# Half of the K tiles of a ConvGLU's gate and value products formed by seven products, with seven operands made once from h

## The chip, the cores and the metric

One core of one Trainium2 chip runs the whole program once per execution. The metric is the device time of that execution in microseconds (us), lower is better. Everything is fp32 at the interface; the matrix products run on TensorE in a reduced fp32 form (fp32r), so each operand is first split into a high part and a low part.

## The reference, cut to what matters

One layer of a hybrid encoder on a sequence of 512 positions with 2048 features. The change touches its last third, the feed-forward network with a convolved gate:

```python
h   = rms_norm(x, norm2_g)                      # (512, 2048)
gv  = h @ ffn_w_up                              # (2048, 2*5504): gate columns, then value columns
g   = dwconv3(gv[..., :5504], dw_w, dw_b)       # width 3 along the positions
val = gv[..., 5504:]
x   = x + (gelu(g) * val) @ ffn_w_down          # (5504, 2048)
return rms_norm(x, final_g)
```

Ahead of it stand a projection, a spatial gating unit, a long convolution by FFT as matrix products, and the output projection `w_out` (`out_group`), whose last two quarters produce x.

## The kernel before, in words

**Products.** `mm3` (L222 to L226) forms one exact product as three matmuls: high by high (L224), high by low (L225, the other way round where the weights stream), low by high (L226). Weights arrive by DMA on SyncE's queue (SP) as raw fp32 tiles of 128x1024 (512 KB, or 384 KB for the last group); ScalarE (ACT) casts each to its high part `hi` (L143), VectorE (DVE) subtracts to get its low part `lo` (L144). `hi` and `lo` have three buffers each, and `next_unit` splits the unit that comes two later when a unit starts (`split_to(i + 3)`), so the split of a unit cannot begin before the unit three places ahead of it has left TensorE (PE), and has to be done two units later.

**Units.** The feed-forward part works in 11 groups of 4 tiles of 128 features (the last has 3). A list, `ffn_order` (L96 to L107), written out by loops, sets the order of the units; PE, ACT, DVE and SP all follow it.

- **R** ("regular"): two K tiles of h times 4 feature tiles of the gate or of the value: 24 matmuls of 512 columns. Eight R units make the gate of one group, eight the value. They accumulate in four PSUM banks `pa`.
- **S**: the product with `ffn_w_down` for the previous group, by a scheme of seven products in place of eight (Strassen's, in Winograd's form): 14 units of 12 matmuls of 512 columns, in two halves of seven. `prepare_to` forms the sums of weight quarters in place on DVE (L180), four buffers `sraw` hold the quarters. The operands `aH`/`aL` are made from the group's activations (`operands`, L1131 to L1169, in three pieces). After each unit `down_out` (L1193) copies two banks to a tile `cs` (ACT, L1199, three buffers) and POOL (GpSimd) issues one DMA, for the fourth unit of a half three, which adds `cs` to the DRAM tile `xd` (L1202, 512 KB each).
- **L**: the last group's product with `ffn_w_down`, direct, at the end.

In a group the R and S units alternate, so that PE gets 5.4 us of R behind nearly every S. Between two gate halves stand `gate_out` (L1121: four DVE multiplications of PSUM by the row `r2`, 1/rms of each position) and the pieces of the convolution (`conv_piece`: ACT L1112, two DVE operations L1113 and L1114, ACT Gelu L1115, and a multiplication by `r2` on POOL, L1116); behind a value half `value_out` (L1128: four DVE multiplications of the gate by PSUM) and the three pieces of `operands`.

**End.** Behind the last R the last S units run, then the L units; `load_fin` (L1280) fetches `xd` back, `last_out` (L1294 to L1297) adds it to the L result, squares and scales it, `leave` writes out.

Of the kernel before, what the change touches and what calls it, by code (L numbers as in the profile page):

```python
# [35 lines left out]
QUARTER = {0: ("11", 0, 0), 1: ("12", 0, 1), 2: ("22", 1, 1), 5: ("21", 1, 0)}  # L36
# [3 lines left out]
    ("11", "22", "11"), ("21", None, None), ("21", "21", "22"),  # L40
)

# [9 lines left out]
def encoder_kernel(ctx: ExitStack, tc: tile.TileContext, a: dict, out: bass.AP):  # L52
# [41 lines left out]

    ffn_order = []
    for gi in range(len(groups)):  # L96
        S = [("S", gi - 1, i // 7, i % 7) for i in range(14)] if gi else []
        G, V = ([("R", kind, gi, k0) for k0 in range(0, KD, 2)] for kind in ("gate", "value"))
        ffn_order += G[:3]
        for i in range(5):  # L100
            ffn_order += S[i : i + 1] + G[3 + i : 4 + i]
        ffn_order += S[5:7]
        late = 2 if gi == last else 0
        for i in range(5 - late):
            ffn_order += V[i : i + 1] + S[7 + i : 8 + i]
        ffn_order += V[5 - late :] + S[12 - late :]
# [40 lines left out]

    def load(i):
        e = plan[i]
        if e[0] == "S":  # L150
            _, gi, dp, u = e
            if u in QUARTER:
                name, ks, dh = QUARTER[u]
                raw = special["raw"]()
                j0, q = groups[gi][0], dp + 2 * dh
                rows = w_dn[j0 * P : (j0 + 4) * P, q * 512 : (q + 1) * 512]
                SP.dma_start(raw, rows.rearrange("(k s p) c -> p s k c", s=2, p=P)[:, ks])
                sraws[gi, dp, name] = raw
# [23 lines left out]

    def split_to(n):
        while st_["split"] < min(n, len(plan)):
# [6 lines left out]
            else:  # L191
                nk, n_ = (2, 512) if plan[i][0] == "S" else (plan[i][2], plan[i][4])
# [644 lines left out]
    xas = [kp.tile([P, 4, L], F32, tag="xa", name="xa", bufs=4) for _ in range(4)]  # L837

    def xa(k):
        return xas[k // 4][:, k % 4, :]  # L840
# [181 lines left out]
    def norm2(q):  # L1022
        H, Lo = h2[q]
        if q == 0:
            ss2s.append(const.tile([P, L], F32, tag="acc", name="ss2", bufs=1))
        ss2 = ss2s[0]
        for f in range(4):
            k = 4 * q + f
            split_scaled(H[:, f, :], Lo[:, f, :], xa(k), col("norm2", k))
            sq = (bo if q < 3 else A3).tile([P, L], F32, tag="ev", name="sq2", bufs=4 if q < 3 else 2)  # L1030
            square_into(ss2, xa(k), sq, k == 0)
# [16 lines left out]
    h2.append(h2_tiles(A2, 0))  # L1048
# [5 lines left out]
    for q in range(1, 4):  # L1054
        go_to(8 * q + 2)
        load_res()
        norm2(q - 1)
        if q < 3:
            h2.append(h2_tiles(A2, q))
# [3 lines left out]
    h2.append(h2_tiles(A3, 3))  # L1063

# [7 lines left out]
    special["raw"] = lambda: ff.tile([P, 2, 512], F32, tag="sraw", name="sraw", bufs=4)  # L1072
# [16 lines left out]
    def turn_x(k):  # L1089
# [6 lines left out]
        if k % 4 == 3:  # L1096
            for t in range(NT):
                SP.dma_start(
                    xd[q, t].rearrange("p (k c) -> p k c", k=4), xas[q][:, :, t * P : (t + 1) * P]
                )  # L1100

    ps_of = {}
    gg = {}
# [4 lines left out]
    def conv_piece(gi, f):  # L1108

        w0, w1, w2_, b = (col(*n(groups[gi][0] + f)) for n in fw)  # L1110
        e, d = gg[gi][:, f, :], tmp[f % 2]
        ACT.activation(d, e, AF.Identity, bias=b, scale=w1)  # L1112
# [319 lines left out]
```

## Time and profile before

| what | value |
|---|---|
| time, median of 3 runs | 2100.76 us (2098.84 to 2101.2) |
| the profiled execution's own time | 2101.48 us |
| its span, first to last instruction | 2099.7 us |
| PE busy | 2065.5 us, 98% of the span |
| DVE busy | 1218.8 us, 58% |
| ACT busy | 898.3 us, 43% |
| POOL busy | 406.7 us, 19% |
| mean granted TensorE clock | 0.995 of full speed |

The span is cut off at the first and last instruction; 1.8 us of the execution's own time lie around it. Busy shares are means over stages with different limits, and matmuls overlap each other in the records, so the time that PE needs for one is read from start to start, not from the recorded length. In every row, "idle" and an arrow name what the engine waited for before the instruction. In the numbers of lines, L1128 is line 1128 of the kernel before.

### The profile page before, as it was taken

What the parts mean: (1) busy time and instruction counts of PE and PEld (TensorE: products, weight loads), DVE (VectorE), ACT (ScalarE), POOL (GpSimd) and SP (SyncE); (2) the same over time, 40 slices, a digit from 0 to 9 for tenths busy, and PEclk for the clock granted to TensorE, in tenths of its full rate; (3) what the DMA queues carried; (4) which work ended last, traced back from release to release, by engine and by line L of the source; (5) the groups of instructions that cost most, each with busy time, mean ns of one, the idle gap of its engine ahead of it and who ended that gap; (6) DMA issues with size and microseconds to landing.
All of it is one profiled execution on the core that took longest, in us unless ns stands there. A gap on an engine that the chain in (4) does not pass through costs nothing.

```text
span 2099.7 us, 23963 instructions
## 1 busy us (share of the span) xinstructions
PE 2065.5 (98%) x9374; PEld 1711.0 (81%) x9374; DVE 1218.8 (58%) x1366; ACT 898.3 (43%) x1230; POOL 406.7 (19%) x304
## 2 busy tenths in 40 slices
PE   8999999999999999999999999999999999999996
PEld 6888887888888888888888888888888888888884
DVE  6873565556897944654555554465555555564555
ACT  6433542223544443543444443443444445344543
POOL 0330211100003510311313122131311213131220
PEclk9999999999999999999999999999999999999998
DMA  8434233243223463887868788786887868788886
GB/s 291 136 120 140 81 91 91 81 140 118 93 91 129 153 180 90 185 190 163 194 143 193 176 181 182 156 195 159 193 189 162 187 153 191 164 188 180 182 195 184
DMA packets 172413, 331.13 MB, mean 158 GB/s; under 512 B 10539, under 2 KB 26091, under 8 KB 170380
## 3 DMA queue, kind: packets, MB, share of 16 engines
q1 hardware_dynamic: 118000, 225.13, 32.9%
q0 software_dynamic: 48960, 94.38, 28.8%
q10 hardware_dynamic: 5340, 10.10, 1.4%
q8 instruction: 73, 1.20, 0.2%
q14 instruction: 40, 0.33, 0.0%
HBM read 222.61 MB, written 106.95 MB: 157 GB/s over the span
## 4 chain that ended last, share of the span: by engine, by line
PE 89%; DVE 6%; DMA 2%; ACT 1%; issue 1%; POOL 0%; SPq 0%; ACTq 0%; POOLq 0%; DVEq 0%
PE pa L224 19%; PE pa L226 19%; PE pa L225 19%; PE po L225 2%; PE po L224 2%; PE po L226 2%; PE se L226 2%; PE se L224 2%; PE se L225 2%; PE sa L226 2%; PE sa L224 2%; PE sa L225 2%; PE sc L226 2%; PE sc L225 2%; PE sc L224 2%; PE pv L224 1%
## 5 line engine op out<-in xcount | busy, mean ns | idle before, releaser
L144 DVE TENSOR_TENSOR lo<-raw,hi 128x1024 fp32r<-128x1024 f32 (+2 forms) x289 | 362.9, 1258 | 403.7 <-ACT hi L143 402.5
L224 PE MATMUL pa<-h2H,hi 128*128 128x512 f32 x1376 | 536.7, 390 | 0.0
L226 PE MATMUL pa<-h2H,lo 128*128 128x512 f32 x1376 | 535.6, 389 | 0.0
L225 PE MATMUL pa<-h2L,hi 128*128 128x512 f32 x1376 | 535.4, 389 | 0.0
L143 ACT CAST hi<-raw 128x1024 fp32r<-128x1024 f32 (+2 forms) x289 | 299.2, 1036 | 386.6 <-PE pa L225 233.4
L1202 POOL DMA_DIRECT2D xd<-cs x180 | 224.6, 1414 | 959.5 <-ACT cs L1199 797.4
L144 DVE TENSOR_TENSOR lo<-sraw,hi 128x1024 fp32r<-128x1024 f32 x140 | 199.0, 1421 | 332.3 <-ACT hi L143 332.2
L143 ACT CAST hi<-sraw 128x1024 fp32r<-128x1024 f32 x140 | 147.2, 1051 | 369.1 <-PE pa L225 367.7
L226 PEld LDWEIGHTS pa<-h2H,lo 128*128 128x128 f32 x1376 | 258.3, 188 | 53.8
L225 PEld LDWEIGHTS pa<-h2L,hi 128*128 128x128 f32 x1376 | 258.3, 188 | 53.3
L224 PEld LDWEIGHTS pa<-h2H,hi 128*128 128x128 f32 x1376 | 258.3, 188 | 53.2
L224 PE MATMUL pa<-hH,hi 128*128 128x512 f32 x512 | 203.3, 397 | 3.5 <-ACT hi L143 1.9
L225 PE MATMUL pa<-hL,hi 128*128 128x512 f32 x512 | 201.4, 393 | 0.0
L226 PE MATMUL pa<-hH,lo 128*128 128x512 f32 x512 | 200.5, 393 | 0.9 <-DVE lo L144 0.9
L224 PEld LDWEIGHTS pa<-hH,hi 128*128 128x128 f32 x512 | 97.1, 190 | 29.6 <-DVE ev L615 4.6
L226 PEld LDWEIGHTS pa<-hH,lo 128*128 128x128 f32 x512 | 97.2, 190 | 22.5 <-DVE lo L144 1.7
L225 PEld LDWEIGHTS pa<-hL,hi 128*128 128x128 f32 x512 | 97.3, 190 | 19.1
L180 DVE TENSOR_TENSOR sraw<-sraw 128x1024 f32<-128x1024 f32 x80 | 99.1, 1239 | 13.0 <-DMA sraw<-in_ffn_w_down 11.0
L1116 POOL TENSOR_TENSOR gg<-gg,r 128x512 f32<-128x512 f32 x43 | 71.6, 1832 | 65.5 <-ACT gg L1115 65.5
L1199 ACT COPY cs<-se 128x512 f32<-128x512 f32 x80 | 47.1, 589 | 51.5 <-PE se L226 51.5
L224 PE MATMUL sa<-hi,aH 128*128 128x512 f32 x160 | 62.2, 389 | 0.0
L225 PE MATMUL sa<-lo,aH 128*128 128x512 f32 x160 | 62.2, 389 | 0.0
(274 smaller groups left out, 3084.2 us busy)
## 6 DMA issues: line engine op xcount, KB each, us to landing
xd<-cs POOLq DMA_DIRECT2D x180, 512.0 KB, 7.8
raw<-in_ffn_w_up SPq DMA_DIRECT2D x160, 512.0 KB, 5.9
sraw<-in_ffn_w_down SPq DMA_DIRECT2D x80, 512.0 KB, 4.6
raw<-in_w_in SPq DMA_DIRECT2D x79, 512.0 KB, 3.7
raw<-in_w_out SPq DMA_DIRECT2D x32, 512.0 KB, 3.7
raw<-in_ffn_w_up SPq DMA_DIRECT2D x16, 384.0 KB, 5.6
xn<-in_xN ACTq DMA_DIRECT2D x8, 512.0 KB, 5.0
khat_d<-kh SPq DMA_DIRECT2D x4, 1024.0 KB, 4.4
```

Of the source, the lines that this page charges most:

```text
L143: ACT.copy(hi, src)
L144: eng.tensor_tensor(lo, src, f32(hi), ALU.subtract)
L180: DVE.tensor_tensor(raws[i], sraws[gi, dp, of], sraws[gi, dp, less], ALU.subtract)
L224: PE.matmul(o, ah, bh, start=start, stop=False, skip_group_check=read)
L225: PE.matmul(o, ah, bl, start=False, stop=False, skip_group_check=read)
L226: PE.matmul(o, al, bh, start=False, stop=stop, skip_group_check=read)
L1116: POOL.tensor_tensor(e, e, r2[0], ALU.mult)
L1199: ACT.copy(st[:, tp, :], chains[dp, CHAIN[u]][tp])
L1202: POOL.dma_start(dst, st, accum_op=ALU.add)
```

## The change

Of the 16 K tiles of h, the first 8 (`KS = 8`) are taken out of the R units. For them gate and value are formed by the same seven-product scheme as the down product, in new units **U**, seven for the gate and seven for the value of each group. A U unit has 24 matmuls (2 feature tiles, 4 K tiles, three each) of 256 columns, where the four R units that it replaces had 96 of 512. The seven operand pairs `hc` are made once from h (`norm2`, `seven`), in part inside `out_group` and in part in the first R units (`first_hook`). The quarters of `ffn_w_up` are loaded as 128x4x256 (512 KB) and summed in place on DVE, in the four buffers that S also uses. Three results go through ACT copies and two DVE additions into a new tile `sums`; the others accumulate in the `pa` banks, with the four R units that are left. `gate_out` is now four additions of `sums` and PSUM, and the multiplication by `r2` a DVE operation of its own (`times`); `value_out` is four additions and two multiplications of 1024 elements. Each half of a group runs its seven U first, then four R with seven S between them. The fifth and sixth S unit trade places, `cs` has two buffers instead of three, and at the end the loads `fin` are issued in another order.

```diff
+KS = 8
     for gi in range(len(groups)):
-        S = [("S", gi - 1, i // 7, i % 7) for i in range(14)] if gi else []
-        G, V = ([("R", kind, gi, k0) for k0 in range(0, KD, 2)] for kind in ("gate", "value"))
-        ffn_order += G[:3]
...
+        for half, kind in enumerate(("gate", "value")):
+            R = [("R", kind, gi, k0) for k0 in range(KS, KD, 2)]
+            U = [("U", kind, gi, u) for u in range(7)]
+            S = [("S", gi - 1, half, u) for u in range(7)] if gi else []
+            if gi == 0:
+                ffn_order += U + R if half else R + U
+                continue
+            ffn_order += U
+            for n, r in zip(((0, 2, 3, 2), (2, 2, 1, 2), (1, 2, 1, 3))[2 if half and gi == last else half], R):
+                ffn_order += [r] + S[:n]
+                S = S[n:]
...
+                    rows = w_up[: KS * P, c0 : c0 + n].rearrange("(j s p) c -> p s j c", s=2, p=P)[:, ks]
...
+        def times(f):
+            DVE.tensor_tensor(g[:, f, :], g[:, f, :], r2[0], ALU.mult)
+
+        def conv(f):
...
+            ACT.activation(d, e, AF.Identity, bias=b, scale=w1)
+            if f + 1 < nf:
+                times(f + 1)
             DVE.scalar_tensor_tensor(d[:, 1:L], e[:, : L - 1], w0, d[:, 1:L], ALU.mult, ALU.add)
             DVE.scalar_tensor_tensor(d[:, : L - 1], e[:, 1:L], w2_, d[:, : L - 1], ALU.mult, ALU.add)
             ACT.activation(e, d, AF.Gelu)
             POOL.tensor_tensor(e, e, r2[0], ALU.mult)
...
     def gate_out(gi):
...
-            DVE.tensor_tensor(gg[gi][:, f, :], o, r2[0], ALU.mult)
-            pieces.append(lambda f=f: conv_piece(gi, f))
+            DVE.tensor_tensor(gg[gi][:, f, :], sm[:, f, :], o, ALU.add)
+        pieces.extend(conv_pieces(gi))
     def value_out(gi):
...
-            DVE.tensor_tensor(g[:, f, :], g[:, f, :], o, ALU.mult)
+            DVE.tensor_tensor(sm[:, f, :], sm[:, f, :], o, ALU.add)
...
+            DVE.tensor_tensor(g[:, fs_, :], g[:, fs_, :], sm[:, fs_, :], ALU.mult)
+    def upper(e):
...
+        for f in range(2):
+            if f >= n2 and u in (1, 2, 5):
+                continue
+            if u in (0, 3, 5, 1):
+                o, new = chains[kind, "b" if u == 1 else "a"][:, f, :], u < 2 and f == 0
+            else:
+                f_ = f + 2 * (u == 2)
+                o, new = ps[f_][:, (first, second)[u == 6]], fresh(kind, gi, f_)
+            for j in range(4):
+                cs = slice(f * P, (f + 1) * P)
+                H, Lo = hc[j // 2]
+                end = j == 3
+                mm3(o, hi[:, j, cs], lo[:, j, cs], H[:, u, j % 2, :], Lo[:, u, j % 2, :], new and j == 0, end, True)
+        def out_0():
+            ACT.copy(sm[:, :2, first], chains[kind, "a"])
+        def out_3():
+            x_ = sm[:, 2:nf, first]
+            ACT.copy(x_, chains[kind, "a"][:, :n2])
+            DVE.tensor_tensor(x_, x_, chains[kind, "b"][:, :n2], ALU.add)
+        def out_5():
+            ACT.copy(sm[:, :2, second], chains[kind, "a"])
+            DVE.tensor_tensor(sm[:, 2:nf, second], sm[:, :n2, second], chains[kind, "b"][:, :n2], ALU.add)
...
-        st = ff.tile([P, 2, 512], F32, tag="cs", name="cs", bufs=3)
+        st = ff.tile([P, 2, 512], F32, tag="cs", name="cs", bufs=2)
...
-    for t in range(NT):
-        load_fin(t)
+    for q in (0, 2):
+        for t in range(2):
+            load_fin(t, q)
     for q in range(4):
         for k0 in range(0, nf, 2):
             next_unit(("L", k0, q), flush)
...
+        for t, q_ in (((0, 1), (1, 1)), ((0, 3), (1, 3)), ((2, 0), (2, 2), (2, 1), (2, 3)), ((3, 0), (3, 2), (3, 1), (3, 3)))[q]:
+            load_fin(t, q_)
```

How the instructions stand on the engines is told by the order of the two programs. DVE's queue where a gate half ends and a value half begins, before (L1121 is `gate_out`, L1113 and L1114 the convolution, L144 a split):

```order
L1121 TENSOR_TENSOR gg<-pa,r_5865 128x512 x3
L1113 SCALAR_TENSOR_TENSOR tmp_5867<-gg,cols,tmp_5867 128x511
L1121 TENSOR_TENSOR gg<-pa,r_5865 128x512
L144 TENSOR_TENSOR lo<-raw,hi 128x1024
L1114 SCALAR_TENSOR_TENSOR tmp_5867<-gg,cols,tmp_5867 128x511
L1113 SCALAR_TENSOR_TENSOR tmp_5868<-gg,cols,tmp_5868 128x511
L1114 SCALAR_TENSOR_TENSOR tmp_5868<-gg,cols,tmp_5868 128x511
L144 TENSOR_TENSOR lo<-sraw,hi 128x1024
```

The same place on DVE in the changed program (L1226 is `gate_out`, L1203 `times`, L1211 and L1212 the convolution, L148 a split, L198 a sum of quarters):

```order
L1226 TENSOR_TENSOR gg<-sums,pa 128x512 x2
L1203 TENSOR_TENSOR gg<-gg,r_5870 128x512
L1226 TENSOR_TENSOR gg<-sums,pa 128x512 x2
L148 TENSOR_TENSOR lo<-sraw,hi 128x1024
L1203 TENSOR_TENSOR gg<-gg,r_5870 128x512
L1211 SCALAR_TENSOR_TENSOR tmp_5872<-gg,cols,tmp_5872 128x511
L1203 TENSOR_TENSOR gg<-gg,r_5870 128x512
L1212 SCALAR_TENSOR_TENSOR tmp_5872<-gg,cols,tmp_5872 128x511
L148 TENSOR_TENSOR lo<-sraw,hi 128x1024
L1211 SCALAR_TENSOR_TENSOR tmp_5873<-gg,cols,tmp_5873 128x511
L1203 TENSOR_TENSOR gg<-gg,r_5870 128x512
L1212 SCALAR_TENSOR_TENSOR tmp_5873<-gg,cols,tmp_5873 128x511
```

Four multiplications by `r2` have come in as rows of their own, and the splits between these rows are now those of U units.

ACT's queue where a value half ends and a gate half begins, in the changed program (`cs` copies are those of S units, `hi` the casts of the units to come, `aH` the operands of the down product, `sums` the copy behind the first U):

```order
L1331 COPY cs<-sc 128x512 x2
L147 CAST hi<-sraw 128x1024
L1331 COPY cs<-sc 128x512
L1048 CAST aH<-gg 128x512 x3
L1048 CAST aH<-tmp_5872 128x512
L1048 CAST aH<-gg 128x512
L1331 COPY cs<-sc 128x512
L147 CAST hi<-sraw 128x1024
L1306 COPY sums<-ua 128x2x256
```

The copies of the sixth and seventh S unit now stand directly ahead of the casts of the second and third U, where before R units were cast.

SP's queue at the end, before:

```order
L1272 DMA grow<-in_final_g 128x2048
L1280 DMA fin<-xd 128x512 x2
L139 DMA raw<-in_ffn_w_down 128x512
L1280 DMA fin<-xd 128x512 x2
L139 DMA raw<-in_ffn_w_down 128x2x512
L139 DMA raw<-in_ffn_w_down 128x512
L139 DMA raw<-in_ffn_w_down 128x2x512
L1280 DMA fin<-xd 128x512 x6
L139 DMA raw<-in_ffn_w_down 128x512
```

And in the changed program:

```order
L1402 DMA grow<-in_final_g 128x2048
L1425 DMA fin<-xd 128x512 x5
L143 DMA raw<-in_ffn_w_down 128x512
L143 DMA raw<-in_ffn_w_down 128x2x512
L1425 DMA fin<-xd 128x512 x2
L143 DMA raw<-in_ffn_w_down 128x512
L143 DMA raw<-in_ffn_w_down 128x2x512
L1425 DMA fin<-xd 128x512
L143 DMA raw<-in_ffn_w_down 128x512
L1425 DMA fin<-xd 128x512 x8
```

The last eight `fin` loads now stand behind the last weights, where six stood ahead of them.

## Rows read from the trace of the kernel before

**Rows 1.** The page, busy time by engine.
```profile
PE 2065.5 (98%) x9374; PEld 1711.0 (81%) x9374; DVE 1218.8 (58%) x1366; ACT 898.3 (43%) x1230; POOL 406.7 (19%) x304
```
**Rows 2.** Windows: each engine's busy time, granted clock, DMA share, GB/s; feed-forward and end.
```profile
840.00:2040.00 1200.00, 1200.00 (x5295) 993.62 (x5294) 644.92 (x632) 532.46 (x714) 269.44 (x215) 1.00 0.80 178
2040.00:2099.70 59.70, 39.53 (x155) 30.89 (x153) 29.14 (x53) 21.84 (x48) 6.12 (x7) 0.87 0.67 190
```
**Rows 3.** Timeline of PE (start, length): matmuls of 512 columns, 18 starts apart.
```profile
999.83 0.39 PE L224 MATMUL sc<-hi,aH 128*128 128x512 f32 x1
...
1003.91 0.39 PE L224 MATMUL pa<-h2H,hi 128*128 128x512 f32 x1
```
**Rows 4.** Timeline of PE: matmuls of 256 columns in the long convolution, 16 starts apart.
```profile
528.97 0.28 PE L225 MATMUL iv<-invL,sH 128*128 128x256 f32 x1
...
530.88 0.28 PE L224 MATMUL iv<-invH,sH 128*128 128x256 f32 x1
```
**Rows 5.** Timeline of DVE behind a value half.
```profile
1055.86 2.73 DVE L1128 TENSOR_TENSOR gg<-gg,pa 128x512 f32<-128x512 f32 x4 [1.34 <-PE pa L226]
1058.62 0.69 DVE L1150 TENSOR_TENSOR tmp<-gg 128x512 f32<-128x512 f32 x1
1059.23 1.22 DVE L144 TENSOR_TENSOR lo<-raw,hi 128x1024 fp32r<-128x1024 f32 x1
1060.37 0.68 DVE L1151 TENSOR_TENSOR gg<-gg 128x512 f32<-128x512 f32 x1
```
**Rows 6.** Timeline of PE: the start of the S unit behind that value half's last R.
```profile
1057.63 0.39 PE L224 MATMUL sg<-hi,aH 128*128 128x512 f32 x1
```
**Rows 7.** Timeline of DVE behind a gate half.
```profile
1122.72 0.75 DVE L1114 SCALAR_TENSOR_TENSOR tmp<-gg,cols,tmp 128x511 f32<-128x511 f32 x1
1123.38 0.75 DVE L1113 SCALAR_TENSOR_TENSOR tmp<-gg,cols,tmp 128x511 f32<-128x511 f32 x1
...
1125.19 3.68 DVE L144 TENSOR_TENSOR lo<-sraw,hi 128x1024 fp32r<-128x1024 f32 x1 [0.28 <-ACT hi L143]
```
**Rows 8.** Timeline of POOL in the same stretch.
```profile
1107.68 3.68 POOL L1202 DMA_DIRECT2D xd<-cs  x3 [6.96 <-ACT cs L1199]
...
1124.75 3.03 POOL L1116 TENSOR_TENSOR gg<-gg,r 128x512 f32<-128x512 f32 x2
...
1132.81 1.28 POOL L1116 TENSOR_TENSOR gg<-gg,r 128x512 f32<-128x512 f32 x1 [3.87 <-ACT gg L1115]
```
**Rows 9.** Groups of DVE by form, 840 to 2040 us: busy, mean ns of one, idle before.
```profile
L144 DVE TENSOR_TENSOR lo<-sraw,hi 128x1024 fp32r<-128x1024 f32 x137 | 195.3, 1426 | 324.6 <-ACT hi L143 324.5
L144 DVE TENSOR_TENSOR lo<-raw,hi 128x1024 fp32r<-128x1024 f32 x139 | 170.5, 1227 | 176.4 <-ACT hi L143 176.4
```
**Rows 10.** Timeline of ACT: an S unit's second copy, then a cast.
```profile
1041.51 0.59 ACT L1199 COPY cs<-sc 128x512 f32<-128x512 f32 x1 [0.77 <-PE sc L226]
1041.99 1.05 ACT L143 CAST hi<-raw 128x1024 fp32r<-128x1024 f32 x1
```
**Rows 11.** The tile xd, 1107 to 1110 us: issue to landing of the three transfers.
```profile
DMA to landing us min/median/max: 5.9/9.9/12.3
```
**Rows 12.** Windows of the end.
```profile
2048.00:2056.00 8.00, 2.83 (x13) 2.06 (x11) 0.27 (x1) 2.24 (x4) 2.40 (x2) 0.83 1.09 281
...
2064.00:2070.00 6.00, 1.82 (x7) 0.94 (x5) 2.52 (x4) 1.34 (x3) 0.00 (x0) 1.00 0.44 144
```
**Rows 13.** Timeline of PE at the end.
```profile
2055.76 0.80 PE L224 MATMUL pl<-lH,laH 128*128 128x512 f32 x1 [5.17 <-ACT lH L143]
...
2058.04 0.63 PE L224 MATMUL pl<-lH,laH 128*128 128x512 f32 x1
2058.46 0.63 PE L225 MATMUL pl<-lL,laH 128*128 128x512 f32 x1
```
**Rows 14.** Timeline of SP's queue at the end.
```profile
2054.94 10.41 SPq L1280 DMA_DIRECT2D fin<-xd  x6
```
**Rows 15.** The page, DMA issues: KB each, median us to landing.
```profile
xd<-cs POOLq DMA_DIRECT2D x180, 512.0 KB, 7.8
```

More of the change, by code (lines that the diff above doesn't have):

```diff
@@ L1020, in load_res, with seven, hi, lo @@
         res.append(t)
-    def norm2(q):
-        H, Lo = h2[q]
-        if q == 0:
-            ss2s.append(const.tile([P, L], F32, tag="acc", name="ss2", bufs=1))
[L1026 to L1031, printed above, removed]
+    def seven(v, H, Lo, s1):
+        v = v.rearrange("p (k s) l -> p s k l", s=2)
+        a11, a12, a21, a22 = (v[:, s, :, h * 256 : (h + 1) * 256] for h in range(2) for s in range(2))
+        def hi(u, src):
+            ACT.copy(H[:, u], src)
+        def lo(u, src):
+            DVE.tensor_tensor(Lo[:, u], src, f32(H[:, u]), ALU.subtract)
+        def first():
+            for u, src in ((0, a11), (4, a12), (6, a22)):
+                hi(u, src)
+            DVE.tensor_tensor(s1, a21, a22, ALU.add)
+            DVE.tensor_tensor(a21, a11, a21, ALU.subtract)
+            lo(0, a11)
+        def second():
+            hi(1, s1)
+            hi(5, a21)
+            for u, src in ((4, a12), (6, a22), (1, s1), (5, a21)):
+                lo(u, src)
+        def third():
+            DVE.tensor_tensor(s1, s1, a11, ALU.subtract)
+            hi(3, s1)
+            DVE.tensor_tensor(a12, a12, s1, ALU.subtract)
+            hi(2, a12)
+            lo(3, s1)
+            lo(2, a12)
+        return [first, second, third]
@@ new lines, in by_two, with hc_tiles, squares, norm2 @@
+    def by_two(t):
+        return t.rearrange("p (k l) -> p k l", k=2)
+    hc = []
+    def hc_tiles(pl, i):
+        return tuple(pl.tile([P, 7, 2, 256], F32R, name=f"hc{n}{i}") for n in "HL")
+    def squares(q, new):
+        if not ss2s:
+            ss2s.append(const.tile([P, L], F32, tag="acc", name="ss2", bufs=1))
+        for k in range(4 * q, 4 * q + 4):
+            square_into(ss2s[0], xa(k), new(), k == 0)
+    def norm2(q, hq, s1, new):
+        if q < 2:
+            for f in range(4):
+                ACT.activation(hq[:, f, :], xa(4 * q + f), AF.Copy, scale=col("norm2", 4 * q + f))
+            steps = seven(hq, *hc[q], s1)
+        else:
+            H, Lo = h2[q]
+            steps = [
+                lambda k=k: split_scaled(H[:, k % 4, :], Lo[:, k % 4, :], xa(k), col("norm2", k))
+                for k in range(4 * q, 4 * q + 4)
+            ]
+        return steps + [lambda: squares(q, new)]
@@ L1170, in regular, with banks_of, fresh, outlet @@
+    def banks_of(kind, gi):
+        if (kind, gi) not in ps_of:
+            ps_of[kind, gi] = [bank("pa") for _ in range(groups[gi][1])]
+        return ps_of[kind, gi]
+    def fresh(*bank_):
+        new = bank_ not in begun
+        begun.add(bank_)
+        return new
+    def outlet(kind, gi, done):
+        if done:
+            posts.append(lambda: (gate_out if kind == "gate" else value_out)(gi))
     def regular(e, hook=None):
@@ L1173, in regular @@
         j0, nf = groups[gi]
-        if k0 == 0:
-            new = sbank if kind == "value" and gi == 0 else bank
-            ps_of[kind, gi] = [new("pa") for _ in range(nf)]
-        ps = ps_of[kind, gi]
         hi, lo = next_unit((w_up, k0, 2, (0 if kind == "gate" else DFF) + j0 * P, nf * P), flush)
+        ps = banks_of(kind, gi)
+        end = gi > 0 or kind == "value"
         for kk in range(2):
@@ L1241, in encoder_kernel @@
             strassen(e)
+        elif e[0] == "U":
+            upper(e)
         else:
@@ L1267, in last_operands @@
     def last_operands():
+        while pieces:
+            piece()
         g = gg.pop(last)
@@ L1285, in encoder_kernel @@
         strassen(e)
-        if "last" in special and e == ("S", last - 1, 1, 4):
+        if e == ("S", last - 1, 1, 4):
             last_operands()
-        piece()
     def last_out(t, q):
```

232 lines of the change are left out of this document (127 added, 105 removed).

## The prediction

> **What bounds the kernel now.** I read the page first, then windows, then timelines. On the page PE is busy for 2065.5 us, 98% of the span [rows 1], and DVE, the next, for 58%. The windows say where: from 840 to 2040 us PE is never idle, at a granted clock of 1.00 (2.4 GHz), beside DVE at 645 of 1200 us and DMA engines busy 80% of the time; only in the last 59.7 us does PE rest, 20 us of it, at a mean clock of 0.87 [rows 2]. So in the feed-forward part time is the number of matmuls times the distance between their starts. That distance is not the recorded length (0.39 us, which overlaps its neighbours): 18 starts of 512 columns lie 4.08 us apart, 0.2267 us each [rows 3]; 16 starts of 256 columns in the long convolution lie 1.91 us apart, 0.1195 us each [rows 4]. A matmul of half the columns costs 0.527 of a whole one.
>
> **What PE saves.** Per half group four R of 24 matmuls go, 96 x 0.2267 = 21.76 us; seven U of 24 come, 168 x 0.1195 = 20.08 us. That is 1.69 us for each of 20 halves, 33.7 us. In the last group 72 x 0.2267 = 16.32 us become 132 x 0.1195 = 15.77 us (its U leave out some tiles), 0.55 us twice. **PE: -34.8 us.** A seventh saved from the count is half eaten by the 0.527.
>
> TensorE: Matmul & The Clock Gate of the Trainium skill, section Back-to-back issue gap, speaks against the change: it says that the load of weights and the matmul together set the spacing, and gives 81 ns at 128 columns and 131 ns at 512. From these figures a matmul of 256 columns would be estimated at some 98 ns, three quarters of a whole one, and the U units would cost 20 x 168 x 0.170 us = 571 us against 435 us for the R. The trace disagrees on both [rows 3, 4], so the sum above stands.
>
> **What must now fit beside PE.** A U unit lasts 24 x 0.1195 = 2.87 us, an R 5.44, an S 2.72. The split of a unit (ACT 1.05 us, DVE 1.14) can start when the unit three places ahead is done and has two units' time. Before, an R gave 5.4 us in nearly every pair; now seven U follow each other, and the work behind a half (`gate_out`, `value_out`) falls into just these. DVE's prices, start to start: 0.61 us for an addition of 512 and 1.14 for 1024 elements [rows 5], 0.66 for a convolution step [rows 7]. I count DVE's rows up to the low part of the fourth U (U3), the last before slack returns. `value_out` starts 1.8 us before the next unit, at 1055.86 against 1057.63 [rows 5, 6]. Then come S5, S6 (5.44) and U0 to U2 (8.61), plus two matmuls (0.24) until the low part is read: 16.1 us.
>
> - Value to gate: four additions (2.4), two products of 1024 (2.28), four splits (4.56), four sums for the operands (2.4), six low parts `aL` (3.6), one sum of quarters (1.14): 16.4 us, 0.3 late. Bounds 0 and 2.5 (some rows wait on ACT).
> - Gate to value: four additions and four `times` (4.8), seven convolution steps (4.6), four splits, one sum: 15.1 us, 1.0 to spare. But POOL's four products lie here too, and while POOL ran two of them (3.03 us) a split on DVE took 3.68 us instead of 1.22 [rows 7, 8]. Splits of S weights, where the products fall, average 1.43 against 1.23 us for the others [rows 9]: 0.2 x 14 = 2.8 us a group. I take 2.6 us of collision, so 1.6 late; bounds 0 and 4.2 (four products of 1.28 us wholly lost to DVE, 5.1 less 1.0).
> - The copies `cs`. With two buffers the copy of the sixth S (S5) waits until all three transfers of S3 have landed. Issued within 1.4 us of each other, the last took 12.3 us [rows 8, 11]: some 14.4 us behind S3's end. In the gate half S5 ends 2.72 + 5.44 + 2.72 = 10.9 us behind S3's end, so its copies start 3.5 late, and ACT, which works in order, holds U1's cast: 3.5 + 1.0 [rows 10] + 1.05 + about 0.9 for the low part, less the 5.6 of S6 and U0: 0.8 us late. In the value half S5 ends 16.3 us behind S3: nothing. This 0.8 lies ahead of the 1.6 at the same transition and is counted from the same start, so it is contained in it. Bounds 0 and 5 (rival 1).
>
> So a group stalls for 0.3 + 1.6 = 1.9 us against 3.37 saved; ten times **+19 us** (bounds 0 and 80). SBUF — State Buffer of the Trainium skill, section SBUF: two separate sides, calls the port that DVE and GpSimd share an exclusive lock held for a whole instruction; the split of 3.68 us agrees. By that rule every product would be lost to DVE, the upper bound of the second point, and the sum would be 26 us more.
>
> **First group.** Value U follow gate U directly, without S and R between: up to U3's split DVE owes four additions, three or four `times`, four convolution steps, two splits and a sum, 10.8 us against 3 x 2.87: 2.3 late. The operands of the second four K tiles are made in the first R units, 11 more DVE rows of 0.61 in 21.8 us; I add nothing for them, 0 to 4 at most. **+2.3 us** (1 to 6).
>
> **The end.** PE waits 5.17 us for a weight cast `lH` [rows 13], because `fin` loads stand ahead of weights in SP's queue: six of them hold it from 2054.94 for 10.41 us, each waiting for the last additions to `xd` [rows 14]. The stretches 2048 to 2056 and 2064 to 2070 have 5.2 and 4.2 us without a matmul [rows 12], and after the first the starts are 0.42 us apart for a while, the lower clock [rows 13]. Now the last weights stand ahead of eight `fin`. I take the 9.4 us as gone less a little: **-9 us**, bounds -3 (the landing of `xd` merely waited for elsewhere) and -12 (clock regained too).
>
> **Sum**, against the profiled execution's own 2101.5 us, 0.7 above the median: -34.8 + 19 + 2.3 - 9 = -22.5, **2079 us**. A difference under 0.2%, 4.2 us, a measurement of this kernel could not tell from none.
>
> **Rivals.**
> 1. *The transfers to xd hold ACT* (slower). S2 and S3 now stand side by side, where before an R lay between, and part of S3's output goes to the same rows of `xd` as S2's; the transfer waits for S2's to land, 7.8 us at the median [rows 15]. If all three wait, the last lands up to 4 us later, 18 behind S3's end, U1's cast waits 4.5 us at PE, and the DVE work behind it is pushed on: with 0.3 and a part of the collision some 6 us a group. 2101.5 - 34.8 + 60 + 2.3 - 9 = 2120. For it: in the changed order only one of the three transfers waits for S2, but DMA engines are at 80% already, and all 9 transfers of a half now fall into the 41 us of R and S of a half of 61. It decides from 4.2 us a group on, where the stalls eat PE's saving and the end. 0.19.
> 2. *POOL's products lock DVE wholly*: 4.2 + 0.3 + 0.8, 5.3 us a group, 2113. Against: the splits' mean excess is 0.2 us, 2.8 a group, not 5.1 [rows 9]. 0.11.
> 3. *The stalls hide*: DVE idles for 46% of the stretch, and the scheduler has spread its rows; stalls under 0.5 us a group, 2060 to 2065. 0.22.
> 4. *The clock falls after stalls*, as after the wait at 2055.76, where starts went to 0.42 us [rows 13]. Two us more a group for the matmuls after each: 2099. Against: waits of 1 to 2 us are far shorter than 5.17. 0.06.
> 5. *A matmul of 256 columns costs more here than in the long convolution*, since other weights come each time there too: excluded by [rows 4] but for 0.01; at 0.13 us the 3624 matmuls are 38 us more, 2117.
> My forecast, stalls of 0.5 to 3.8 us a group (2065 to 2097), has 0.41.
>
> **Range.** The likeliest case gives 2065 to 2097. Rivals 3, 1 and 2 carry it to 2056 (no stalls, end -12, first group 1) and to 2126. Faster: the forecast but for its last edge, and rival 3, 0.62; same, 2097 to 2106, that edge and rival 4, 0.07; slower, rivals 1, 2 and 5, 0.31.
>
> **What would show it.** U's starts 0.12 us apart with PE gap-free inside the later U of a half; short idle on PE ahead of U1 to U3 behind gate halves, put down to DVE `lo`; no wait ahead of `pl` at the end. Wrong: PE idle ahead of U1 put down to ACT's cast, behind `cs` copies that waited for `xd` (rival 1); splits of 2 to 4 us beside POOL's products in each group (rival 2); a lower granted clock between 840 and 2000 us (rival 4).

## The result

| kernel | time, median us (range, runs) | span | granted clock |
|---|---|---|---|
| before | 2100.98 (2098.84 to 2101.78, 4) | 2099.7 | 0.995 |
| changed | 2219.43 (2216.75 to 2223.29, 4) | 2219.6 | 0.973 |

The ratio is 1.0567, with a 95% interval from 1.0547 to 1.0587: the change costs 5.7%, where I had forecast a gain of 1% and a range that ended at 2126. Page of the changed kernel, the span and the rows that answer to [rows 1]:

```profile
span 2219.6 us, 27650 instructions
...
PE 2075.8 (94%) x10934; PEld 1779.8 (80%) x10934; DVE 1471.9 (66%) x1643; ACT 1002.7 (45%) x1376; POOL 416.6 (19%) x308
```

PE is busy 94% of a longer span instead of 98%. Its windows, as [rows 2] (engines' busy time, granted clock, DMA share, GB/s):

```profile
860.00:2160.00 1300.00, 1202.45 (x6599) 1046.18 (x6599) 852.34 (x855) 614.30 (x824) 280.49 (x220) 0.96 0.74 163
2160.00:2219.60 59.60, 40.89 (x170) 32.71 (x168) 34.55 (x60) 25.80 (x55) 5.82 (x7) 0.87 0.73 209
```

In the stretch where PE had not rested at all it now rests for 98 of 1300 us, at a mean clock of 0.96 instead of 1.00. What it waits for there (total us, times, longest):

```profile
PE sc L242 <- ACT cs L1331: 78.7, 18, 8.1
PE ua L244 <- DVE lo L148: 9.3, 18, 0.8
PE ua L242 <- ACT sums L1310: 4.5, 9, 0.6
```

One wait stands out: `sc`, the bank of the sixth and seventh S unit, for ACT's copy `cs`. To place it, I cut the program at four starts read from PE's timeline. "Group 1" begins at the first S less the R or U units ahead of it (before: three R, 16.3 us; changed: seven U and two R, 31.0). In the changed kernel the first U of group 1 really starts 2.3 us earlier, so 2.3 us of group 0's +10.0 are waits inside group 1's first U units.

| stretch | before | changed | difference |
|---|---|---|---|
| up to the first matmul of the feed-forward part | 716.4 | 722.1 | +5.8 |
| group 0 | 96.5 | 106.5 | +10.0 |
| groups 1 to 10, up to the last S matmul's start | 1229.2 | 1346.0 | +116.8 |
| the rest | 57.7 | 44.9 | -12.7 |

In groups 1 to 10 the matmuls alone, at the prediction's distances, take 9 x (336 x 0.1195 + 360 x 0.2267) + 102 = 1198 us. So 148 us of waits and slow matmuls stand there, where I had written 19. Read from start to start of the matmuls, 112 of them stand at S units and 35 at U units.

**The wait.** PE's timeline in a gate half of the changed kernel, the last matmul of S5 and the first of S6:

```profile
1292.61 0.39 PE L244 MATMUL sc<-hi,aL 128*128 128x512 f32 x1
1301.09 0.79 PE L242 MATMUL sc<-hi,aH 128*128 128x512 f32 x1 [8.09 <-ACT cs L1331]
1301.68 0.63 PE L243 MATMUL sc<-lo,aH 128*128 128x512 f32 x1
1302.11 0.63 PE L244 MATMUL sc<-hi,aL 128*128 128x512 f32 x1
```

S6 adds onto the two banks that S5 has just filled, so its first matmul waits until ACT has copied them out. ACT's timeline tells why the copy is late:

```profile
1282.16 0.59 ACT L1331 COPY cs<-sa 128x512 f32<-128x512 f32 x1 [0.70 <-PE sa L244]
...
1290.17 1.08 ACT L1331 COPY cs<-sg 128x512 f32<-128x512 f32 x2 [6.48 <-DMA xd<-cs]
...
1300.45 1.07 ACT L1331 COPY cs<-sc 128x512 f32<-128x512 f32 x2 [4.36 <-DMA xd<-cs]
```

The rows are the second copy of S3, the copies of S4, and those of S5. With two buffers S4's copies wait for S2's transfer and S5's for S3's. POOL's timeline, the issues of S2, of S3 (one, then two) and of S4:

```profile
1280.33 1.20 POOL L1334 DMA_DIRECT2D xd<-cs  x1 [6.62 <-ACT cs L1331]
1283.05 1.20 POOL L1334 DMA_DIRECT2D xd<-cs  x1 [1.52 <-ACT cs L1331]
1290.36 3.68 POOL L1334 DMA_DIRECT2D xd<-cs  x3 [6.11 <-DMA xd<-cs]
```

S3's second transfer writes where S2's does and waits for it to land; the last of the three lets S5's copy start at 1300.45, 18.3 us behind the start of S3's last copy at 1282.16. S5's last matmul ended 10.7 us behind it. Such a wait, of 6.4 to 8.1 us, stands in all ten gate halves and in the last value half; in the other value halves, where S5 ends later, it is at most 1.0. In the kernel before, the units S4, S5 and S6 used the banks `c`, `g`, `c`; the change made that `g`, `c`, `c`, so that nothing stands between the two uses of `c`.

**The clock.** The two slow rows behind the wait are no accident. Window behind it:

```profile
1301.10:1306.00 4.90, 4.90 (x12) 3.84 (x13) 3.15 (x4) 3.20 (x5) 1.83 (x2) 0.50 0.98 163
```

The granted clock is 0.50 (1.2 GHz) after 8 us without a matmul, and twelve matmuls start 0.43 us apart instead of 0.23: 2.4 us more here. Over the eleven waits of 6.4 to 8.1 us it is 1.4 to 2.6 us each, 23 in all; the clock is back at 1.00 some 3 to 6 us after the restart. It falls behind shorter waits too. From 2048 us on PE waits 0.78, 0.76, 1.41 and 0.76 us in U units. The third of these waits, and a window behind the fourth:

```profile
2052.52 0.38 PE L242 MATMUL ua<-hcH,hi 128*128 128x256 f32 x1 [1.41 <-ACT hi L147]
```

```profile
2054.50:2057.50 3.00, 3.00 (x17) 3.00 (x16) 3.00 (x3) 0.00 (x0) 0.00 (x0) 0.50 0.03 12
```

Behind the single waits of 0.5 to 1.0 us on `sc` in the value halves it stayed at 1.00.

### The profile page after: what moved, and what is told of

Same layout as the page of the kernel before. It is cut to its first block, busy times and chain, and to the rows that moved or that the text cites. A ratio compares the mean times of both kernels' runs of the same rounds, so it can differ in the third digit from the quotient of the medians.

```text
span 2219.6 us, 27650 instructions
## 1 busy us (share of the span) xinstructions
PE 2075.8 (94%) x10934; PEld 1779.8 (80%) x10934; DVE 1471.9 (66%) x1643; ACT 1002.7 (45%) x1376; POOL 416.6 (19%) x308
## 4 chain that ended last, share of the span: by engine, by line
PE 61%; DVE 15%; DMA 11%; issue 6%; ACT 4%; POOL 2%; ACTq 0%; SPq 0%; POOLq 0%; DVEq 0%
PE pa L242 10%; PE pa L244 10%; PE pa L243 10%; DMA xd<-cs 8%; DVE lo L148 4%; PE ua L244 2%; DVE sraw L198 2%; PE ua L242 2%; PE ua L243 2%; PE po L244 2%; PE se L244 2%; PE se L242 2%; PE se L243 2%; PE po L242 2%; PE po L243 2%
## 5 line engine op out<-in xcount | busy, mean ns | idle before, releaser
L148 DVE TENSOR_TENSOR lo<-sraw,hi 128x1024 fp32r<-128x1024 f32 x294 | 358.6, 1225 | 272.3 <-ACT hi L147 271.7
L148 DVE TENSOR_TENSOR lo<-raw,hi 128x1024 fp32r<-128x1024 f32 (+2 forms) x201 | 254.3, 1268 | 282.7 <-ACT hi L147 281.9
L147 ACT CAST hi<-sraw 128x1024 fp32r<-128x1024 f32 x294 | 307.3, 1052 | 283.8 <-PE pa L243 173.2
L198 DVE TENSOR_TENSOR sraw<-sraw 128x1024 f32<-128x1024 f32 x168 | 224.6, 1346 | 83.8 <-DMA sraw<-in_ffn_w_up 80.2
L242 PE MATMUL pa<-h2H,hi 128*128 128x512 f32 x688 | 269.6, 392 | 0.2 <-ACT hi L147 0.2
L243 PE MATMUL pa<-h2L,hi 128*128 128x512 f32 x688 | 268.5, 390 | 0.0
L244 PE MATMUL pa<-h2H,lo 128*128 128x512 f32 x688 | 267.9, 390 | 0.0
L244 PE MATMUL ua<-hcH,lo 128*128 128x256 f32 x520 | 151.3, 291 | 12.0 <-DVE lo L148 12.0
L242 PE MATMUL ua<-hcH,hi 128*128 128x256 f32 x520 | 151.5, 291 | 8.4 <-ACT sums L1310 4.5
L243 PE MATMUL ua<-hcL,hi 128*128 128x256 f32 x520 | 149.2, 287 | 0.0
L242 PE MATMUL pa<-hcH,hi 128*128 128x256 f32 x520 | 147.5, 284 | 1.7 <-ACT hi L147 1.7
L243 PE MATMUL pa<-hcL,hi 128*128 128x256 f32 x520 | 147.1, 283 | 0.0
```

Of the source, the lines that this page charges most:

```text
L147: ACT.copy(hi, src)
L148: eng.tensor_tensor(lo, src, f32(hi), ALU.subtract)
L198: DVE.tensor_tensor(raws[i], sraws[key, of], sraws[key, less], ALU.subtract)
L242: PE.matmul(o, ah, bh, start=start, stop=False, skip_group_check=read)
L243: PE.matmul(o, ah, bl, start=False, stop=False, skip_group_check=read)
L244: PE.matmul(o, al, bh, start=False, stop=stop, skip_group_check=read)
```

## The experiments

Each kernel below was run beside the kernel before (2099.6 to 2100.6 us in these runs). "Groups" is the stretch of groups 1 to 10 of the table above, cut in the same way; matmuls alone are 1198.

| run | edit | time, us | ratio to before | groups |
|---|---|---|---|---|
| changed | | 2219.4 | 1.0567 [1.0547, 1.0587] | 1346 |
| e1 | three buffers `cs` | 2174.3 | 1.0351 [1.0337, 1.0365] | 1292 |
| e2 | S spread as in the value half | 2152.6 | 1.0244 [1.0230, 1.0258] | 1274 |
| e3 | an R between S2 and S3 | 2215.6 | 1.0535 [1.0515, 1.0555] | |
| e4 | the kernel before, new end only | 2099.1 | 0.9993 [0.9984, 1.0002] | |
| e5 | e1 and e2 | 2135.3 | 1.0171 [1.0155, 1.0188] | 1252 |
| e6 | e5 without POOL's products | 2101.9 | 1.0008 [0.9998, 1.0017] | 1224 |
| e7 | e5, pieces written behind R and S | 2120.5 | 1.0102 [1.0082, 1.0122] | 1245 |
| e8 | e7, and issued there | 2094.8 | 0.9970 [0.9960, 0.9980] | 1221 |
| e9 | e8, own buffer for `hq0` | 2086.9 | 0.9941 [0.9927, 0.9954] | 1218 |
| e10 | e5, products on DVE | 2126.4 | 1.0121 [1.0106, 1.0136] | 1245 |
| e11 | e9 with two buffers `cs` | 2127.2 | 1.0125 [1.0108, 1.0142] | 1267 |

### e1: three buffers

```diff
-        st = ff.tile([P, 2, 512], F32, tag="cs", name="cs", bufs=2)
+        st = ff.tile([P, 2, 512], F32, tag="cs", name="cs", bufs=3)
```

> The changed kernel with three buffers for the copies cs instead of two, nothing else. In its trace PE waits about 7.5 us in each gate half ahead of the seventh S unit (S6) for ACT's copy of the sixth (S5), which waits for a cs buffer, that is for the last of S3's three transfers to land. Theory 1 (the buffer count): with three buffers S5's copy takes the buffer of S2, whose transfer has landed some 3 us before S5 ends; the 7.5 us and the 2.4 us of half clock behind them go in each of 10 groups, and about 0.7 in the value halves: 2219 - 105 = about 2115 us, and the wait of PE on sc for ACT cs falls from 86 us to under 10. Theory 2 (the DMA queue is simply full): the wait moves on to the next copy and to U's casts, at least half of it stays, over 2165 us. Theory 3 (DVE's bursts): what the 8 us had hidden behind gate halves comes out as waits for lo of 1.6 to 5 us a group, 2130 to 2165.

45 us came back, not 105. PE's wait on `sc` is gone from the list, and U units wait in its place:

```profile
PE ua L244 <- DVE lo L148: 15.6, 24, 0.9
PE pa L244 <- DVE lo L148: 14.4, 15, 1.3
PE pa L242 <- ACT hi L147: 13.4, 10, 2.0
PE ua L242 <- ACT hi L147: 8.3, 7, 1.7
...
ACT cs L1331 <- DMA xd<-cs: 47.2, 10, 5.2
```

The last row (of ACT) is the reason: S6's copy now needs S3's buffer, waits 5 us in each of ten gate halves and holds the casts of U units behind it. This is the wait that the prediction had priced, one S unit later. Theories 2 and 3 both hold in part: the wait moved, and DVE's burst came out. From start to start 93 of the 94 us over the matmuls' 1198 now stand at U units, and in nine of the ten groups the granted clock falls to 0.50 behind two to four waits of 0.7 to 2.0 us that follow each other.

### e2: S earlier in the gate half

```diff
-            for n, r in zip(((0, 2, 3, 2), (2, 2, 1, 2), (1, 2, 1, 3))[2 if half and gi == last else half], R):
+            for n, r in zip(((2, 2, 1, 2), (2, 2, 1, 2), (1, 2, 1, 3))[2 if half and gi == last else half], R):
```

> The changed kernel, with the S units of the gate half spread as those of the value half: (2, 2, 1, 2) S behind the four R instead of (0, 2, 3, 2); cs keeps two buffers. S5 then ends 16.3 us behind S3 instead of 10.9. Theory 1 (the landing of S3's transfers, 18 us behind S3's end, holds S5's copy and so S6): the wait in gate halves falls to that of the value halves, 0.7 us, in 9 of 10 groups; 2219 - 9 x (6.8 + 2.4) = about 2135 us, less what DVE then shows. Theory 2 (full queue): the landing moves with S3, over 2180 us.

The order alone takes off 67 us, 17 short of the estimate. PE's waits of this kernel:

```profile
PE sc L242 <- ACT cs L1331: 20.1, 15, 7.0
PE ua L244 <- DVE lo L148: 15.2, 26, 0.9
PE ua L242 <- ACT sums L1310: 7.3, 8, 0.9
```

On `sc` 20.1 us are left of 78.7, 7 of them in the last half, whose order was not changed. In these 18 halves the last of S3's transfers still lands 15 to 17 us behind S3, so the distance from S3 to S5 against the landing decides, as theory 1 had it; most of the rest stands at U units.

### e3: S2 and S3 apart

```diff
-            for n, r in zip(((0, 2, 3, 2), (2, 2, 1, 2), (1, 2, 1, 3))[2 if half and gi == last else half], R):
+            for n, r in zip(((0, 3, 2, 2), (2, 2, 1, 2), (1, 2, 1, 3))[2 if half and gi == last else half], R):
```

> The changed kernel, with (0, 3, 2, 2) S behind the four R of the gate half: an R now lies between S2 and S3, while S5 still ends 10.9 us behind S3. It tells the two causes of the late landing apart. If the wait of S3's second transfer for S2's landing (6.1 us on POOL) is what delays it, the three land some 14.4 us behind S3's end, S6 waits about 4 us instead of 7.5 in each gate half and the time falls by 30 to 50 us, to 2170 to 2190. If the three transfers take 18 us in any case because the DMA engines are full, nothing changes: 2210 to 2225.

2215.6 us: hardly a change, and so the number of the second reading. A half like the one above, POOL's issues, ACT's copies of S5 and the wait of S6 there:

```profile
1281.29 4.92 POOL L1334 DMA_DIRECT2D xd<-cs  x4 [5.33 <-issue]
...
1293.96 1.07 ACT L1331 COPY cs<-sc 128x512 f32<-128x512 f32 x2 [5.18 <-DMA xd<-cs]
...
1294.60 0.80 PE L242 MATMUL sc<-hi,aH 128*128 128x512 f32 x1 [6.15 <-ACT cs L1331]
```

The edit did not take the wait for S2's landing away. S2's transfer lands at 1280.78, and POOL issues nothing until then: the wait now stands ahead of the first of S3's three transfers instead of the second. The three go out together with S4's, the DMA share of 1281 to 1295 is 1.07, and the last of the three lands 11.1 us after its issue, 16.5 behind S3's end. Over nine gate halves S3's second and third transfer went out some 2 us earlier behind S3 than in the changed kernel, and the last landed 17.1 us behind S3's end instead of 17.6. Issuing them earlier is worth little while the engines are that busy; when they would land without any wait for S2's transfer, no run shows.

### e4: the new end alone

In the kernel before, the `fin` loads were split by quarter and issued in the change's order, and `grow` loaded ahead:

```diff
-    for t in range(NT):
-        load_fin(t)
+    for q in (0, 2):
+        for t in range(2):
+            load_fin(t, q)
...
+        for t, q_ in (((0, 1), (1, 1)), ((0, 3), (1, 3)), ((2, 0), (2, 2), (2, 1), (2, 3)), ((3, 0), (3, 2), (3, 1), (3, 3)))[q]:
+            load_fin(t, q_)
```

> The kernel before with the new order of the end alone (fin loads split by quarter and issued between and behind the last weights, grow loaded earlier). Prediction's term: -9 us, bounds -3 and -12: 2089 to 2098, with 2092 the likeliest. Rival: the end waits for the landing of xd anyway, within 3 us of before.

1.5 us less, with an interval that holds zero: the rival. PE's wait for weight casts at the end did fall, to 4.9 us from 9.3. SP's queue, and two pieces of the chain of work that ended last:

```profile
2045.91 7.51 SPq L1280 DMA_DIRECT2D fin<-xd  x3
2053.52 0.41 SPq L139 DMA_DIRECT2D raw<-in_ffn_w_down  x1
2057.93 5.17 SPq L1280 DMA_DIRECT2D fin<-xd  x4
```

```profile
2039.95 12.33 DMA raw<-in_ffn_w_down
2053.52 8.64 DMA raw<-in_ffn_w_down
```

The loads still wait for `xd`, in two places instead of one. The chain runs over two loads of the last weights and then through some 33 us of, in the main, additions, squares and scalings (`last_out`), where before it ran over the landing of `xd` (14.3 us) and of `fin` (9.4).

The 12.7 us that the changed kernel gains behind its last S are the other side of S6's wait: from S5's end (2162.9, when S6 could have started) to the end of the span are 56.7 us, against 60.2 in the kernel before. In the later kernels where S6 hardly waits (e1, e5 to e10), the stretch behind the start of the last S matmul takes 51.5 to 52.0 us, against 57.7 before and 56.8 in e4. There the end does gain 6 us. The last transfer to `xd` lands 15 us behind that start in e5 and e9, and 22 us behind it before and in e4. In these kernels three S units stand behind the last R, where there were four. No run tells this order of the S units from the order of the loads.

### e5: both mends of the copies

> The changed kernel with three buffers cs and the S units of gate halves spread as (2, 2, 1, 2): both earlier edits together. The spread alone gave 2152.6 us with 22 us of PE waits left on the copies cs; the buffer alone 2174.3, where the copy of the last S then waited for S3's transfers instead and held ACT. Theory 1 (the two mend different waits: S5's copy waits no more, and S3's transfers have landed before the seventh copy needs the third buffer): the 22 us go, 2125 to 2135, and what is left of PE's waits are lo, hi and sums of U units. Theory 2 (transfers to xd fill the queue whatever the order): no better than 2150.

Theory 1. The waits on `cs` fall to under 2 us, and 54 us are left over the matmuls' 1198, 51 of them at U units. That is 5.4 us a group, where I had counted 1.9. The longest in PE's list:

```profile
PE ua L244 <- DVE lo L148: 14.6, 23, 0.9
PE ua L242 <- ACT hi L147: 7.7, 7, 2.5
PE ua L242 <- ACT sums L1310: 4.5, 5, 0.9
```

### e6 and e10: POOL's products

```diff
-            POOL.tensor_tensor(e, e, r2[0], ALU.mult)
```

> e5 without the multiplication by r2 on POOL behind Gelu (it leaves this factor out of the output). It measures what POOL's four products a group cost through DVE. In the trace of the spread alone the DVE rows beside them were 3 to 4 us longer a group (steps of 2.05 and 1.77 us instead of 0.74, sums of quarters 3.45 for two instead of 2.4). Theory 1 (these reach PE): 20 to 36 us under e5. Theory 2 (the bursts are bound by the number of rows and the chain sum, cast, low part): within 8 us of e5.

33 us less than e5. DVE's rows of the feed-forward part are some 40 us shorter in all, 30 of them in the convolution's steps and 10 in sums of quarters, so about four fifths of what POOL's products cost DVE reaches PE. Groups of DVE, 860 to 2040 us, in e5 and then in e6 (the steps of the convolution):

```profile
L1211 DVE SCALAR_TENSOR_TENSOR tmp<-gg,cols,tmp 128x511 f32<-128x511 f32 x39 | 45.7, 1173 | 0.0
L1212 DVE SCALAR_TENSOR_TENSOR tmp<-gg,cols,tmp 128x511 f32<-128x511 f32 x39 | 42.4, 1088 | 0.0
```

```profile
L1212 DVE SCALAR_TENSOR_TENSOR tmp<-gg,cols,tmp 128x511 f32<-128x511 f32 x39 | 29.1, 747 | 0.0
L1211 DVE SCALAR_TENSOR_TENSOR tmp<-gg,cols,tmp 128x511 f32<-128x511 f32 x39 | 29.1, 747 | 0.0
```

The means of e5 mix two kinds: 29 of the 78 steps took 1.76 to 1.80 us, the others 0.73 to 0.76 as in e6. SBUF — State Buffer of the Trainium skill, section SBUF: two separate sides, speaks of one port shared by DVE and GpSimd as an exclusive lock; these rows agree: a step that meets a product takes 1.04 us longer, and a product alone takes 1.28 us [rows 8].

e10 put the products on DVE instead (`DVE.tensor_tensor` in the same place).

> e5 (2135.3 us) with the four products by r2 behind Gelu on DVE instead of POOL; nothing is left out. It adds four rows of 0.61 us, 2.4 us a group, to DVE, the engine that is late, and takes POOL out. Theory 1 (what hurts is that POOL's product stretches DVE's rows beside it, 30 us or so in all as e6 showed, with products of 1.3 to 1.8 us): between e6 and e5 by the price of the rows, 2102 + up to 24 = 2105 to 2126. Theory 2 (the products hurt by being late themselves, as value_out waits for them, or by POOL's queue of transfers): as e5, 2130 or more.

2126.4, at the upper edge of theory 1: 24 us of rows came for 33 of collisions, and no step of DVE is stretched any more. Here the rows on DVE itself cost as much time as they last. The two theories lie only 4 us apart at this edge, so the run speaks for the first and does not rule out a part of the second.

### e7 to e9: the work moved out of the burst

e7 gave POOL's products pieces of their own and ran pieces behind R and S only:

```diff
-        piece()
+        if e[0] != "U" or (e[1] == "gate" and e[3] >= 4):
+            piece()
```

> e5 with the convolution's pieces (their times rows, two steps, Gelu) and POOL's products kept out of the U units: they run behind R and S units only, the products last; the operands of the down product are made from the fifth U of a gate half on. Nothing is left out. Theory (what falls into the U burst of a value half is what stalls it): the waits of PE on lo, hi and sums in U units fall to under 2 us a group, and the time to 30 to 45 us under e5, 2085 to 2105. Rival (U units stall by themselves, since sum, cast and low part of a quarter take 3.4 us in a chain against 2.87 us of a unit): at least half of the waits stay, 2115 or more.

15 us less than e5: a number in the rival's range, but no proof of it, since the edit did not do what I meant. DVE's timeline in e7, inside a U burst:

```profile
1386.08 1.79 DVE L1212 SCALAR_TENSOR_TENSOR tmp<-gg,cols,tmp 128x511 f32<-128x511 f32 x1
1387.79 1.21 DVE L148 TENSOR_TENSOR lo<-sraw,hi 128x1024 fp32r<-128x1024 f32 x1
1388.92 1.79 DVE L1211 SCALAR_TENSOR_TENSOR tmp<-gg,cols,tmp 128x511 f32<-128x511 f32 x1
```

The convolution still stands between the splits of U, and beside POOL's products: the scheduler had moved it back up. e8 ties every piece in the order of issue behind the split issued last on DVE, and the cast on ACT, and lets it run only in the half that it belongs to:

```diff
     def piece():
         if pieces:
-            pieces.pop(0)()
+            with tc.issue_after(getattr(st_["act"], "ins", st_["act"])), tc.issue_after(getattr(st_["dve"], "ins", st_["dve"])):
+                pieces.pop(0)()
...
-        if e[0] != "U" or (e[1] == "gate" and e[3] >= 4):
+        half = e[1] if e[0] != "S" else ("gate", "value")[e[2]]
+        if half == st_["half"] and (e[0] != "U" or (half == "gate" and e[3] >= 4)):
             piece()
```

> e5 with the work behind a half really moved out of the U units. In e7 the scheduler had hoisted the convolution back: its steps and POOL's first products still stood between the splits of U units. Here each piece is tied, in the order of issue alone, behind the split that was issued last, and runs only behind R and S units of the value half (convolution, products) or from the fifth U of the gate half on (operands of the down product); nothing is left out. In DVE's order a U burst then holds four additions, splits and sums only. Theory (bursts stall PE by the rows of the half before them, lengthened by POOL): groups 1 to 10 take 1200 to 1215 us instead of e5's 1252, 2085 to 2100 in all. Rival (the chain sum, cast, low part of a U quarter stalls PE in any case): groups stay above 1230 us, 2110 or more.

2094.8: the same work, 40 us less than e5, and groups of 1221 us, a little above the forecast. PE's waits in e8:

```profile
PE sc L243 <- DVE lo L148: 10.2, 8, 2.8
...
PE ua L244 <- DVE lo L148: 0.5, 1, 0.5
```

The waits at U units are all but gone, so sum, cast and low part do not stall them by themselves. Of the 23 us that are left over the matmuls, 15 stand at S units, which now wait for DVE in the halves that took the work. This kernel is 0.3% faster than before.

e9 mends the start. In the changed kernel `hq0`, four scaled K tiles of h, lies in the buffer of the residual `res`, so the next residual loads late; POOL waits for it, and PE behind DVE (changed kernel, POOL's and PE's timelines):

```profile
676.16 2.54 POOL L1030 TENSOR_TENSOR tb<-tb,res 128x512 f32<-128x512 f32 x2 [8.10 <-DMA res<-in_xT]
```

```profile
687.45 0.79 PE L244 MATMUL po<-ybH,lo 128*128 128x512 f32 x1 [5.12 <-DVE lo L148]
```

The edit, beside the smaller `ev`:

```diff
-    hq0 = bo.tile([P, 4, L], F32, tag="res", name="hq0", bufs=1)
+    hq0 = bo.tile([P, 4, L], F32, name="hq0")
+    load_res()
```

> e8, and the scaled first K tiles (hq0) get a buffer of their own. In the changed kernel hq0 lies in the buffer of the residual res, so the residual of the second quarter loads only when the seven operands are made; POOL then waits 8 us for it, and PE 5.3 us for a split that stands behind the additions on DVE's queue. To make room the buffers ev go from four to three and the four additions of a quarter are made two by two. Theory (that shared buffer costs the 5 us ahead of the feed-forward part): 3 to 6 us under e8. Rival (DVE's rows there cost it, or the pairs of additions hold PSUM banks longer): no change or up to 5 us more.

The feed-forward part starts at 714.2 us instead of e8's 722.7, and the time is 2086.9, 7.9 under e8, more than the theory gave, and **0.6% faster than the kernel before**. POOL's wait for `res` is gone and so is PE's of 5.12 us. Its page and PE's waits from 640 to 2100 us:

```profile
PE 2036.2 (98%) x10934; PEld 1756.1 (84%) x10934; DVE 1462.8 (70%) x1643; ACT 1004.8 (48%) x1376; POOL 414.3 (20%) x308
```

```profile
PE sc L243 <- DVE lo L148: 8.0, 8, 2.0
PE pl L242 <- ACT lH L147: 3.9, 2, 2.5
```

The span of e9's profiled execution is 18.6 us shorter than that of the kernel before (the medians differ by 14.1). Of this, 10.8 us lie in groups 1 to 10 and 6.0 in the end. The 2.2 ahead of the feed-forward part are what the code of the kernel before varies by itself: that kernel starts the part at 716.4 us, and e4, the same up to there, at 714.0.

### e11: e9 with two buffers again

> e9 (2086.9 us) with two buffers cs, as in the changed kernel. S5 ends 16.3 us behind S3 in both halves now, but in the last half, spread as (1, 2, 1, 3), 10.9. Theory (S5's copy needs S3's last transfer, 16 to 18.5 us behind S3): PE waits 0.7 to 1.5 us in each of 18 halves and some 7 in the last two, 2086.9 + 20 to 35 = 2107 to 2122. Rival (with the U bursts freed, the transfers land earlier): within 8 us of e9.

40 us more than e9, with this row in PE's waits:

```profile
PE sc L242 <- ACT cs L1337: 36.0, 18, 6.8
```

That is 2 us a half, more than expected. The extra lies in the value halves, which took the work moved out of the bursts: there S3's last transfer lands 18 to 20 us behind S3, against 16 to 17 in the gate halves, and S6 waits 1.8 to 3.1 us instead of 1.0 at most. Behind six of these nine waits the granted clock fell to 0.50 as well. What makes the transfers late there is open. The third buffer is worth 40 us once the bursts are mended.

## Why the prediction was wrong

- **PE's saving (-34.8 us) was right.** The U matmuls start 0.12 us apart. From PE's timeline of the changed kernel, 18 starts apart, as [rows 4]:

```profile
1173.75 0.28 PE L244 MATMUL ub<-hcH,lo 128*128 128x256 f32 x1
...
1175.91 0.28 PE L244 MATMUL ub<-hcH,lo 128*128 128x256 f32 x1
```

  In e9 groups 1 to 10 take 1218 us against 1229 before, with some 20 us of waits and slow matmuls left, 14 of them at S units: 1198 for the matmuls themselves.
- **The copies `cs`: the step that failed.** I had the buffer, the transfer and the distance of 10.9 us, and put the price at the wrong place. I followed ACT's queue to U1's cast, which has 5.6 us of slack, and did not ask who else waits for the copy: S6, next in PE's order, on the same PSUM banks (`CHAIN` "aeeagcc" had put the two uses of `c` side by side), with no slack at all. The size was off too: in the gate halves the last of S3's transfers lands 16.7 to 18.4 us behind S3's end and not 14.4. So a term that I had put at nothing of its own, contained in another, cost 112 us with the slow clock behind it. Rival 1 had that landing, and the same place wrong; with the right one it gives 18 - 10.9 = 7.1 us, and 6.4 to 8.1 were measured. Whether the old order of the fifth and sixth S unit would have been a mend by itself was not tried.
- **The clock: rival 4, at 0.06.** It came as part of the above: 1.4 to 2.6 us behind each wait of 6 to 8 us, about as priced, but for other waits than those it was priced for. What I held against it, that waits of 1 to 2 us are far shorter than 5.17, was no safe argument: the clock fell behind 1.41 us at 2052.5 too, and in nine groups of e1.
- **DVE beside the U bursts: right mechanism, wrong size.** 1.9 us a group were forecast, 5.4 measured in e5. I had taken 1.0 us of slack and the 2.6 us by which splits were longer before; but 33 us, 3.3 a group, go with POOL's products alone, near rival 2's price (4.2, at 0.11). In the changed program the products fall beside convolution steps and sums of quarters (1.35 us on average, 1.22 in e6) and hardly beside splits (1.23 and 1.22). The other 2.1 go when the rest of the half's work leaves the burst (e8). That the 1.0 us of slack was missing because I had added up DVE's rows alone, while ACT's cast stands between a sum and its low part, is my reading; no run tests it. A wait that I had not listed is that of U5, which accumulates onto U3's bank, for the copy to `sums`. DVE's wait for quarters of the gate and value weights (80 us in 20 times) I had not listed either; in e9 DVE still waits 52 us for them, and PE's list has no wait of a U unit for DVE, so there at least it does not reach PE.
- **First group, +2.3 us: 11 to 13 measured** (10.0 over before by the cut above, 7.7 by the real start of group 1, where PE's own time is 3.4 less). The transposes of x now come in pairs and wait for ACT (2.7 and 1.0 us at one place), and U units of both kinds follow each other. In e9, with the half's work out of the bursts, group 0 takes 96.9 us, 0.4 over before.
- **The operands made inside `out_group`: a term left out.** The 0 to 4 us of the prediction were for those made in the first R units. Ahead of the feed-forward part 5.8 us came, not by DVE's rows but by the shared buffer (e9, which also makes the additions two by two).
- **The end, -9 us: -1.5 measured** for the order of the loads alone (e4). PE's idle time there was a symptom: it fell by 4.4 us and the work behind it ended hardly sooner. In e1 and e5 to e10 the end takes 6 us less than before, inside the bounds of -3 and -12, but there the S units of the last half stand in another order too, and `xd` has landed sooner; that I had not reasoned.

## What to carry to other kernels

When a buffer count goes down, list every consumer of what the buffer drains, PE's next accumulation onto the same banks first, and price the wait at the one with the least slack. A burst of short units wants the engine that feeds it free of the previous stage's work, and free of a neighbour that stretches its rows; here the same work, moved out of the burst, was worth 40 us. Look at the built order after such a move: the scheduler may have undone it.

## What the runs showed of the hardware

After 6 to 8 us without a matmul PE restarts at a granted clock of 0.50 for 3 to 6 us, at 0.43 us per matmul of 512 columns; the eleven such waits of the changed kernel, 81 us, cost 23 us more behind them. The clock also fell behind waits of 1.2 to 2.0 us that had others of 0.7 to 1.3 close by (nine groups of e1), and behind six of the nine waits of 1.8 to 3.1 us in e11. A matmul of 256 columns with a fresh load of weights each time holds 0.12 us over whole units. And a convolution step of 0.75 us on DVE takes 1.78 where it meets a product on POOL; taking POOL's products out of e5 gave 33 us, against the 34.8 by which PE's own work had become shorter.
